# Moving the long sequence's Fourier mixing of a two-sequence encoder block to the start of the short sequence's gate and up products, through DRAM

## The chip, the cores and the metric

One core of one Trainium2 chip runs the kernel. The time is the device time of one execution in microseconds (us). TensorE does the matmuls, ScalarE (ACT in the profile), VectorE (DVE) and GpSimd (POOL) work on elements, and SyncE (SP) issues nearly all of the kernel's transfers, in one queue.

## The reference, cut to what matters

```python
def fourier_mix(u, w_fnet):            # u: (batch, positions, 512), 4 groups of 128 channels
    ug = u.reshape(b, s, FNET_GROUPS, FNET_GROUP_DIM)
    fr = jnp.fft.fftn(ug, axes=(1, 3), norm="ortho").real
    return jnp.einsum('bsgc,gcd->bsgd', fr, w_fnet).reshape(b, s, FNET_WIDTH)

def trunk(x, ...):
    h = rmsnorm(x, g_pre_mix[l])
    p = h @ w_in[l]                    # c_q | c_kv | k_rope | f_in
    a = mla(c_q, c_kv, k_rope, g_q[l], w_uq[l], g_kv[l], w_ukv[l])
    f = fourier_mix(f_in, w_fnet[l])
    mix = jnp.concatenate([a, f], axis=-1) @ w_out[l]
    x = x + rmsnorm(mix, g_post_mix[l])
    h = rmsnorm(x, g_pre_ffn[l])
    x = x + rmsnorm(conv_ffn(h, w_gate[l], w_up[l], conv_w[l], conv_b[l], w_down[l]), g_post_ffn[l])
    return x

def reference(x_prompt, x_sample, ...):   # (1, 1024, 1024) and (1, 512, 1024), float32
    return trunk(x_prompt, ...), trunk(x_sample, ...)
```

The two requests share the weights and nothing else. The model width is 1024, there are 8 heads, and the feed-forward width is 2816.

## The kernel before, in words

The request of 1024 positions is called long, that of 512 short. Every float32 product is three matmuls of halves: `split` (L103 to L105) rounds a tile to fp32r on ACT (the `hi` half) and subtracts it from the tile on POOL or DVE (the `lo` half); hi times hi, hi times lo and lo times hi are summed in PSUM. So each operand costs one cast of ACT and one subtraction of POOL or DVE before TensorE can use it. All tiles live in one pool of 51 pages of 4 KB a partition (`pg`); PSUM has four one-bank tiles (`ps1`) and two two-bank tiles (`ps2`). The program is written in one order of Python calls; the Tile framework then sets each engine's order of instructions from it with a scheduler of its own, and puts in the waits. Each engine runs its instructions in that order. SP issues loads and stores in its order as well, and a load or store that has to wait holds up those behind it.

The program goes through these stages.

1. Input projection of short and of the two halves of long (`in_products`, L231). `in_finish` (L240) leaves long's Fourier input folded: `fs` and `fd`, the sums and differences of mirrored positions, two pages each (L267, L268). Short's Fourier mixing runs between the blocks of the last part (`between0` to `between3`).
2. The preparation of attention: `key_rope`, the load of `w_ukv` and `w_uq`, their splits (`prep_attention_kv`, `prep_attention_q` with sixteen small copies that rearrange the heads, L452 to L455), the values of short (`attention_values`, L472 to L474, `pv`, `vc`).
3. **Long's Fourier mixing.** Three tables `tr` are loaded (`fourier_load`) and split into `th`, `tl`; `fourier_fold` (L334) makes `ff` on POOL; `fourier_operand` splits `fd` and `ff` into `eh`, `el`. For each of four channel groups, `fourier_positions` (L350 to L352, `py`) multiplies by the tables, `yh` and `yl` (L371, L372) split the result, and `fourier_channels` (L383 to L385, `pv`, `pu`, `px`) multiplies by the group's matrices A and B (`abh`, `abl`); L394 to L405 put the output `fT` together, which is stored to `mixT` in DRAM. `prep_attention_q` and `attention_keys` are called after the second of these steps.
4. Attention of short and then of long (`scores`, L541; the maximum `mx` of a block, L544, is the first thing that DVE does with a block's scores), with `w_out` loaded and split during long's last heads (`wload`, `wsplit`, list `wo`), and short's output projection (`mix_short`) at its end.
5. Short's gate and up products: 22 units (`ShortGateUp.unit`, L777), each a gate product and an up product of 24 matmuls of 512 columns. A weight is loaded and split three products ahead (`AHEAD`), gate weights on POOL and up weights on DVE. The dictionary `steps` puts other work ahead of a unit: step 1 loads the first half of long's mixed activations (`mix_load`, four tiles `mtr`), step 2 splits them (`mth`, `mtl`), steps 3 to 6 are long's eight blocks of the output projection (L674, `pm`), steps 8 to 19 make and split the left operands of long's gate and up products.
6. Long's gate and up products (`LongGateUp`, L858) and the down products of both (`Down`, L1003).

Of the kernel before, what the change touches and what calls it, by code (L numbers as in the profile page):

```python
# [9 lines left out]
F32 = mybir.dt.float32  # L10
# [34 lines left out]
def kernel(  # L45
# [41 lines left out]
    def store(dst, src):  # L87
        nc.sync.dma_start(dst, src)
# [67 lines left out]
    def seq(x, y, S, tdft, name):  # L156
        q = Ctx()
        q.x, q.y, q.S, q.tdft, q.name = x[0], y[0], S, tdft, name
        q.C = S // 512
        q.KB = S // P  # L160
        q.mixT = dr.tile([D, S], F32, name=f"mixT_{name}")
        q.x1 = dr.tile([S, D], F32, name=f"x1_{name}")
        q.c = [[None] * q.C for _ in range(4)]
        q.kr = None
        q.vc, q.ks, q.qt = {}, [], {}
        q.xf = {}
        q.fold, q.traw, q.tab, q.ops = {}, {}, {}, {}
        return q


# [69 lines left out]
    def in_finish(q, c, b, o, cb):  # L240
        pc, pf = o
        if b % 2 == 0:
            cb.page = pg([P, 2, 512], F32, "cn")
        cn = cb.page[:, b % 2, :]
        ss = small("ss2", 2)
        for i in range(2):
            hs = slice(i * LORA, (i + 1) * LORA)
            nc.scalar.activation(cn[:, hs], pc[:, hs], AF.Square, accum_out=ss[:, i:i + 1])
        r = rstd(ss, LORA, 2)
        for i in range(2):  # L250
            hs = slice(i * LORA, (i + 1) * LORA)
            nc.vector.tensor_scalar(out=cn[:, hs], in0=pc[:, hs], scalar1=r[:, i:i + 1], scalar2=None, op0=ALU.mult)
        cb.append(cn)
        tb = c * 4 + b
        half = q.KB // 2
        if tb < half:
            if tb % 2 == 0:
                q.xf[tb // 2] = pg([P, 2, 512], F32, "xf")
            nc.scalar.copy(q.xf[tb // 2][:, tb % 2, :], pf)
        else:  # L260
            n = tb - half
            xf = q.xf[n // 2][:, n % 2, :]
            i, j = n // 2, n % 2
            if j == 0:
                q.fold["s", i] = pg([P, 2, 512], F32, "fs")
                q.fold["d", i] = pg([P, 2, 512], F32, "fd")
            nc.vector.tensor_tensor(out=q.fold["s", i][:, j, :], in0=pf, in1=xf, op=ALU.add)  # L267
            nc.vector.tensor_tensor(out=q.fold["d", i][:, j, :], in0=xf, in1=pf, op=ALU.subtract)  # L268

    def key_rope(q, c, w, hT, cs4):  # L270
        pk = ps1("pk")
# [18 lines left out]

    def prep_fourier():

        w = Ctx()
        tb = pg([P, 2, P], F32, "dft")
        load(tb, t_dft.rearrange("t p c -> p t c"))
        wf = pg([P, GROUPS, P], F32, "wf")
        load(wf, w_fnet.rearrange("g p c -> p g c"))
        raw = pg([P, 2, GROUPS * P], F32, "abr")
        for i in range(2):
            pa = ps1("pa")  # L300
            mm(pa, tb[:, i, :], wf.rearrange("p g c -> p (g c)"), start=True, stop=True)
            nc.scalar.copy(raw[:, i, :], pa)
        w.hi = pg([P, 2, GROUPS * P], F32R, "abh")
        w.lo = pg([P, 2, GROUPS * P], F32R, "abl")
        split(w.hi, w.lo, raw)
        return w

    def fourier_load(q, n):
        raw = pg([P, 2, q.tdft.shape[3]], F32, "tr")
# [860 lines left out]
    def between2():  # L1170
        for f in fs[3:7]:
            f()
        load_attention(wkvr, w_ukv, NOPE + 64)
        for n in (0, 2):
            fourier_load(long, n)

    def between3():
        fourier_fold(long)
        fs[7]()

    wf, wkvr, wqr = [], [], []
# [1 line left out]
    for i, (q, c) in enumerate(chunks):  # L1183
# [27 lines left out]
            transpose_c(q, c, cb)  # L1211
        km = key_rope(q, c, win, cur, cs4)
        prev = (q, c, cb, km)
    fourier_load(long, 1)
    load_attention(wqr, w_uq, NOPE + ROPE)
    wa = Ctx()
    prep_attention_kv(wa, wkvr)
    fourier_table(long, 0)
    fourier_operand(long, ("d", 0))
    fourier_table(long, 2)  # L1220
    for key in "eo":
        fourier_operand(long, key)
    attention_values(short, wa)
    key_rope_finish(prev[0], prev[1], prev[3])
    fourier_table(long, 1)
    fourier_operand(long, ("d", 1))
    for i, f in enumerate(fourier_steps(long, wf[0])):
        f()
        if i == 1:
            prep_attention_q(wa, wqr)  # L1230
            attention_keys(short)
    project_k(short, wa, 0)
    project_q(short, wa, ORDER[0])
    gb1 = broadcast_gain(g_post_mix)
# [41 lines left out]

    hb = ([], [])
    steps = {}
    steps[1] = [lambda: box.update(mr=mix_load(long, 0))]
    steps[2] = [lambda: box.update(mt=mix_operands(box["mr"]))]  # L1280

    def blocks(c, bs):
        for b in bs:
# [5 lines left out]
        box["mt"] = mix_operands(raws)  # L1289
        hb[0].append(out_finish(long, 0, 3, pm, gb1))  # L1290

    steps[3] = [lambda: blocks(0, range(2))]
    steps[4] = [lambda: blocks(0, (2,)), last_block]
    steps[5] = [lambda: blocks(1, range(2))]
    steps[6] = [lambda: blocks(1, range(2, 4))]
    for kk in range(4):
        steps[8 + 3 * kk] = [lambda kk=kk: gu_long.left(kk, hb)]
        steps[9 + 3 * kk] = [lambda kk=kk: gu_long.left_operands(kk, slice(0, 4))]
        steps[10 + 3 * kk] = [lambda kk=kk: gu_long.left_operands(kk, slice(4, 7))]
    steps.setdefault(NJ - 2, []).append(lambda: gu_long.fetch(0))  # L1300
    steps.setdefault(NJ - 1, []).extend([lambda: [f() for f in gu_long.weight_steps(0)], lambda: gu_long.fetch(1)])
    for j in range(NJ):
# [74 lines left out]
```

## Time and profile before

| | |
|---|---|
| Time, median of 3 runs | 1695.25 us (1695.03 to 1699.75) |
| The profiled execution | 1696.39 us, of which its span is 1694.6 us |
| TensorE busy | 1653.6 us of the span (98%) |
| VectorE, GpSimd, ScalarE busy | 1045.6, 900.6 and 751.8 us (62%, 53%, 44%) |
| Chain that ended last | 87% TensorE, 4% VectorE, 3% issue, 2% ScalarE, 2% GpSimd, 1% DMA |
| Moved | 193.38 MB, 114 GB/s on the mean |

The profile is of one execution. Busy time of an engine is the time in which it had an instruction under way. The start of each instruction, what it waited for, and the granted clock of TensorE in a stretch (1.00 is 2.4 GHz; at the lower level, 1.2 GHz, a row shows 0.50 or, where the stretch takes in some of both, a value between) come from the same trace. Line numbers are those of the kernel before.

### The profile page before, as it was taken

The page shows a single profiled execution, that of the slowest core. Times are in us where ns is not written, and L with a number is a line of the kernel's source. Part 1 is how long each engine was busy: PE and PEld are TensorE (multiplying, and loading weights), DVE is VectorE, ACT ScalarE, POOL GpSimd, SP SyncE. Part 2 cuts the span into 40 slices and gives each one's busy share as a digit, 9 for nine tenths or more (in the row PEclk, how much of TensorE's full clock was granted, in tenths as well). Part 3 has the DMA queues.
Part 4 walks back from the last instruction along what each step waited for, and adds up shares of the span by engine and source line. Part 5 has one row for each costly group of instructions (what it writes and reads, how often), then busy time and mean ns, then how long its engine had stood idle before and what let it go on. Part 6 is the DMA issues. An engine that isn't in the chain of part 4 may idle for free.

```text
span 1694.6 us, 21125 instructions
## 1 busy us (share of the span) xinstructions
PE 1653.6 (98%) x7686; PEld 1359.1 (80%) x7686; DVE 1045.6 (62%) x1242; ACT 751.8 (44%) x1274; POOL 900.6 (53%) x646
## 2 busy tenths in 40 slices
PE   8999889999999999999999999999999999999998
PEld 6888767788887777888888888888888887888886
DVE  4333768878887454434666576676667669723547
ACT  5332546666777343323444334333333335532432
POOL 3111436768778413311443777777777626635755
PEclk9999999999999999999999999999999999999999
DMA  6000310000003344535344434333344467645536
GB/s 242 26 8 14 131 63 10 13 11 10 22 23 131 106 128 127 178 97 146 112 126 126 125 93 118 100 94 97 103 119 117 138 214 263 217 147 190 199 132 248
DMA packets 170717, 193.38 MB, mean 114 GB/s; under 512 B 9994, under 2 KB 120822, under 8 KB 170614
## 3 DMA queue, kind: packets, MB, share of 16 engines
q1 hardware_dynamic: 169654, 190.21, 35.7%
q10 hardware_dynamic: 960, 1.84, 0.3%
q8 instruction: 60, 0.98, 0.2%
q14 instruction: 43, 0.35, 0.1%
HBM read 142.86 MB, written 49.15 MB: 113 GB/s over the span
## 4 chain that ended last, share of the span: by engine, by line
PE 87%; DVE 4%; issue 3%; ACT 2%; POOL 2%; DMA 1%; DVEq 0%; SPq 0%; POOLq 0%; ACTq 0%
PE po L1003 16%; PE pm L674 8%; PE pc L231 8%; PE mx L858 7%; PE mz L858 7%; PE my L858 7%; PE gate L777 7%; PE up L777 7%; PE sc L541 5%; PE mv L858 4%; PE pt L553 3%; PE pa L561 2%; PE pa L562 2%; ACT pr L545 1%; DVE pT L556 1%
## 5 line engine op out<-in xcount | busy, mean ns | idle before, releaser
L1003 PE MATMUL po<-bw,aw 128*128 128x512 f32 x924 | 219.7, 390 | 0.0
L1003 PEld LDWEIGHTS po<-bw,aw 128*128 128x128 f32 x924 | 173.4, 188 | 36.0
L142 POOL TENSOR_TENSOR r<-v,mhalf 128x1 f32<-128x1 f32 (+1 forms) x60 | 40.0, 669 | 260.6 <-DVE v L140 260.5
L548 POOL TENSOR_TENSOR pr<-pr,rs 128x1024 f32<-128x1024 f32 (+1 forms) x96 | 155.6, 1622 | 7.1
L858 PE MATMUL my<-hl,wx 128*128 128x512 f32 x528 | 128.6, 389 | 0.0
L858 PE MATMUL mz<-hl,wx 128*128 128x512 f32 x528 | 126.9, 389 | 0.0
L858 PE MATMUL mx<-hl,wx 128*128 128x512 f32 x528 | 126.9, 389 | 0.0
L105 POOL TENSOR_TENSOR wl<-wr,wh 128x1024 fp32r<-128x1024 f32 x22 | 53.9, 2449 | 131.1 <-ACT wh L104 125.6
L105 POOL TENSOR_TENSOR wx<-wr,wx 128x512 fp32r<-128x512 f32 x44 | 75.9, 1725 | 88.5 <-ACT wx L104 88.4
L556 DVE TENSOR_TENSOR pT<-pt,pT 128x512 fp32r<-128x512 f32 x160 | 104.9, 684 | 25.0 <-ACT pT L555 23.4
L105 DVE TENSOR_TENSOR aw<-raw,aw 128x1024 fp32r<-128x1024 f32 (+1 forms) x41 | 65.2, 1589 | 89.4 <-ACT aw L104 67.5
L1003 PE MATMUL po<-bw,an 128*128 128x512 f32 x462 | 115.9, 390 | 1.2 <-POOL bw L105 0.7
L858 PEld LDWEIGHTS my<-hl,wx 128*128 128x128 f32 x528 | 99.2, 188 | 20.5
L858 PEld LDWEIGHTS mx<-hl,wx 128*128 128x128 f32 x528 | 99.1, 188 | 20.5
L858 PEld LDWEIGHTS mz<-hl,wx 128*128 128x128 f32 x528 | 99.1, 188 | 20.5
L544 DVE TENSOR_REDUCE mx<-sc 128x1 f32<-128x1024 f32 (+1 forms) x96 | 99.3, 1041 | 23.5 <-PE sc L541 23.0
L777 PE MATMUL gate<-h2T,wh 128*128 128x512 f32 x352 | 110.9, 393 | 0.0
L105 POOL TENSOR_TENSOR bw<-rb,bw 128x512 fp32r<-128x512 f32 x44 | 71.7, 1647 | 69.6 <-ACT bw L104 69.5
L777 PE MATMUL up<-h2T,wh 128*128 128x512 f32 x352 | 108.4, 389 | 0.0
L555 ACT CAST pT<-pt 128x512 fp32r<-128x512 f32 x160 | 90.1, 590 | 39.6 <-PE pt L553 38.4
L231 PE MATMUL pc<-winh,hT 128*128 128x512 f32 x368 | 106.1, 399 | 1.1 <-ACT hT L217 0.5
L547 POOL TENSOR_TENSOR rs<-sm,mone 128x1 f32<-128x1 f32 x96 | 60.1, 627 | 88.2 <-ACT pr L545 83.4
(262 smaller groups left out, 3965.3 us busy)
## 6 DMA issues: line engine op xcount, KB each, us to landing
wr<-in_w_gate_dram SPq DMA_DIRECT2D x44, 512.0 KB, 4.2
wr<-in_w_up_dram SPq DMA_DIRECT2D x44, 512.0 KB, 6.0
raw<-left SPq DMA_DIRECT2D x76, 256.0 KB, 3.8
rb<-in_w_down_dram SPq DMA_DIRECT2D x55, 256.0 KB, 4.0
rb<-in_w_down_dram SPq DMA_DIRECT2D x22, 512.0 KB, 5.1
left<-sa SPq DMA_DIRECT2D x20, 512.0 KB
ran<-left SPq DMA_DIRECT2D x77, 128.0 KB, 3.6
xb<-in_x_prompt_dram SPq DMA_DIRECT2D x16, 512.0 KB, 5.4
```

The source lines that it names most:

```text
L105: (lo_eng or nc.gpsimd).tensor_tensor(out=lo, in0=src, in1=f32(hi), op=ALU.subtract)
L231: mm(o[i], hT[k][:, part, s], ww[:, i * 512:(i + 1) * 512], start=(k == 0 and part == 0 and ww is wh), stop=(k == KT - 1 and part == 1))
L541: mm(sc[:, hs], st[:, s], mv[:, hs], start=a, stop=z)
L544: nc.vector.tensor_reduce(out=mx, in_=sc[:, 0:S], op=ALU.max, axis=AX.X, negate=True)
L547: nc.gpsimd.tensor_tensor(out=rs, in0=sm, in1=mone, op=ALU.pow)
L548: nc.gpsimd.tensor_tensor(out=pr, in0=pr, in1=rs.to_broadcast([P, S]), op=ALU.mult)
L555: nc.scalar.copy(t[:, 0, :], pt)
L556: nc.vector.tensor_tensor(out=t[:, 1, :], in0=pt, in1=f32(t[:, 0, :]), op=ALU.subtract)
L674: mm(pm[:, hs], st[:, s], mv[:, hs], start=(k == 0 and st is ah and mv is wh), stop=(k == KT - 1 and st is al))
L777: mm(o, st[:, k, :], self.q.h2[k][0][:, part, :], start=(k == 0 and st is hi and part == 0), stop=(k == KT - 1 and st is lo))
L858: mm(o, w[:, wp, s], a[:, ap, :], start=(start and kk == 0 and wp == 0 and ap == 0), stop=(stop and kk == 3 and wp == 1), skip_group_check ...
L1003: mm(o, st[:, s], w[:, wp, :], start=(start and st is ah and wp == 0), stop=(stop and st is al), skip_group_check=True)
```

## The change

Long's folded Fourier input (four pages) and the product `raw` of the channel matrices are stored to DRAM when they are made. Long's Fourier mixing is taken out of the place between the preparation of attention and attention; `prep_attention_q` and `attention_keys` follow the values directly. Ahead of unit 0 of short's gate and up products the four folded pages (`fr`), the channel matrices (`abr`) and the three tables (`tr`) are loaded, eight transfers of 512 KB, and their folds and splits are called; two, three and three of the eight Fourier steps (four position and four channel products) stand ahead of units 1, 2 and 3. The split halves of `w_out` are given up after short's projection, and `w_out` is loaded and split a second time at steps 3 to 7. Long's mixed activations are loaded at step 6 instead of 1 and split at 7 instead of 2, the eight blocks of the output projection stand at steps 8 to 11 instead of 3 to 6, and the left operands at steps 12 to 19, two steps for each of four parts instead of three. In the new numbering L366 to L368 are the position products, L488 to L490 the values, L690 `pm` and L793 the gate and up products.

```diff
...
         q.fold, q.traw, q.tab, q.ops = {}, {}, {}, {}
+        q.kept = dr.tile([q.KB // 2, P, 1024], F32, name=f"fold_{name}")
         return q
...
             nc.vector.tensor_tensor(out=q.fold["d", i][:, j, :], in0=xf, in1=pf, op=ALU.subtract)
+            if j and q.C == 2:
+                for z, key in enumerate("sd"):
+                    store(q.kept[2 * z + i], q.fold.pop((key, i)).rearrange("p j c -> p (j c)"))

...

-        w = Ctx()
         tb = pg([P, 2, P], F32, "dft")
...
             nc.scalar.copy(raw[:, i, :], pa)
+        store(kept_ab, raw.rearrange("p i c -> p (i c)"))
+        return fourier_channel_operands(raw)
+
+    def fourier_channel_operands(raw):
+        w = Ctx()
         w.hi = pg([P, 2, GROUPS * P], F32R, "abh")
...
         return w
+
+    kept_ab = dr.tile([P, 2 * GROUPS * P], F32, name="kept_ab")
+
+    def fourier_reload(q):
+        for z, key in enumerate("sd"):
+            for i in range(2):
+                t = q.fold[key, i] = pg([P, 2, 512], F32, "fr")
+                load(t.rearrange("p j c -> p (j c)"), q.kept[2 * z + i])

...
         load_attention(wkvr, w_ukv, NOPE + 64)
-        for n in (0, 2):
-            fourier_load(long, n)

     def between3():
-        fourier_fold(long)
         fs[7]()
...
         prev = (q, c, cb, km)
-    fourier_load(long, 1)
     load_attention(wqr, w_uq, NOPE + ROPE)
     wa = Ctx()
     prep_attention_kv(wa, wkvr)
-    fourier_table(long, 0)
-    fourier_operand(long, ("d", 0))
-    fourier_table(long, 2)
-    for key in "eo":
-        fourier_operand(long, key)
     attention_values(short, wa)
     key_rope_finish(prev[0], prev[1], prev[3])
-    fourier_table(long, 1)
-    fourier_operand(long, ("d", 1))
-    for i, f in enumerate(fourier_steps(long, wf[0])):
-        f()
-        if i == 1:
-            prep_attention_q(wa, wqr)
-            attention_keys(short)
+    prep_attention_q(wa, wqr)
+    attention_keys(short)
     project_k(short, wa, 0)
...
     steps = {}
-    steps[1] = [lambda: box.update(mr=mix_load(long, 0))]
-    steps[2] = [lambda: box.update(mt=mix_operands(box["mr"]))]
+
+    def fourier_begin():
+        fourier_reload(long)
+        box["ab"] = pg([P, 2, GROUPS * P], F32, "abr")
+        load(box["ab"].rearrange("p i c -> p (i c)"), kept_ab)
+        for n in (0, 2, 1):
+            fourier_load(long, n)
+
+    def fourier_first():
+        fourier_fold(long)
+        fourier_table(long, 0, nc.vector)
+        fourier_operand(long, ("d", 0))
+        fourier_table(long, 2)
+        for key in "eo":
+            fourier_operand(long, key)
+
+    def fourier_second():
+        fourier_table(long, 1)
+        fourier_operand(long, ("d", 1))
+        box["fs"] = fourier_steps(long, fourier_channel_operands(box["ab"]))
+
+    def fourier_go(n):
+        for f in box["fs"][n]:
+            f()
+
+    def wout_load(ks):
+        for k in ks:
+            wload(k)
+
+    def wout_split(ks):
+        for k in ks:
+            wsplit(k)
+
+    steps[0] = [fourier_begin, fourier_first, fourier_second, lambda: wo.clear()]
+    steps[1] = [lambda: fourier_go(slice(0, 2))]
+    steps[2] = [lambda: fourier_go(slice(2, 5))]
+    steps[3] = [lambda: fourier_go(slice(5, 8))]
+    for k in range(0, KT, 2):
+        steps.setdefault(3 + k // 2, []).append(lambda k=k: wout_load((k, k + 1)))
+        steps[4 + k // 2] = [lambda k=k: wout_split((k, k + 1))]
+    steps[6].append(lambda: box.update(mr=mix_load(long, 0)))
+    steps[7].append(lambda: box.update(mt=mix_operands(box["mr"])))

...

-    steps[3] = [lambda: blocks(0, range(2))]
-    steps[4] = [lambda: blocks(0, (2,)), last_block]
-    steps[5] = [lambda: blocks(1, range(2))]
-    steps[6] = [lambda: blocks(1, range(2, 4))]
+    steps[8] = [lambda: blocks(0, range(2))]
+    steps[9] = [lambda: blocks(0, (2,)), last_block]
+    steps[10] = [lambda: blocks(1, range(2))]
+    steps[11] = [lambda: blocks(1, range(2, 4))]
     for kk in range(4):
-        steps[8 + 3 * kk] = [lambda kk=kk: gu_long.left(kk, hb)]
-        steps[9 + 3 * kk] = [lambda kk=kk: gu_long.left_operands(kk, slice(0, 4))]
-        steps[10 + 3 * kk] = [lambda kk=kk: gu_long.left_operands(kk, slice(4, 7))]
+        steps[12 + 2 * kk] = [lambda kk=kk: gu_long.left(kk, hb), lambda kk=kk: gu_long.left_operands(kk, slice(0, 3))]
+        steps[13 + 2 * kk] = [lambda kk=kk: gu_long.left_operands(kk, slice(3, 7))]
     steps.setdefault(NJ - 2, []).append(lambda: gu_long.fetch(0))
...
```

The framework's scheduler places the instructions anew. Three places follow.

**After the values of short, on DVE.** `wv` are the halves of the value weights, `vc` the values, `el` the lower halves of long's Fourier operands, `yl` those of the position products, `wqa` the rearranged query weights. Before:

```order
L105 TENSOR_TENSOR wv_1623<-wqkvr_1472,wv_1623 128x512
L105 TENSOR_TENSOR wv_1631<-wqkvr_1474,wv_1631 128x512
L105 TENSOR_TENSOR el_1644<-fd_1131,eh_1643 128x1024
L105 TENSOR_TENSOR el_1652<-ff_1540,eh_1651 128x1024
L105 TENSOR_TENSOR el_1656<-ff_1542,eh_1655 128x1024
L478 TENSOR_TENSOR vc_1666<-pv_1659,vc_1666 128x4x128
L478 TENSOR_TENSOR vc_1676<-pv_1669,vc_1676 128x4x128
L478 TENSOR_TENSOR vc_1686<-pv_1679,vc_1686 128x4x128
L478 TENSOR_TENSOR vc_1696<-pv_1689,vc_1696 128x4x128
L105 TENSOR_TENSOR el_1707<-fd_1385,eh_1706 128x1024
L372 TENSOR_TENSOR yl_1711<-py_1712,yh_1710 128x2x2x128
L372 TENSOR_TENSOR yl_1711<-py_1713,yh_1710 128x2x256
```

With the change:

```order
L105 TENSOR_TENSOR wv_1621<-wqkvr_1478,wv_1621 128x512
L105 TENSOR_TENSOR wv_1629<-wqkvr_1480,wv_1629 128x512
L494 TENSOR_TENSOR vc_1644<-pv_1637,vc_1644 128x4x128
L494 TENSOR_TENSOR vc_1654<-pv_1647,vc_1654 128x4x128
L468 COPY wqa_1680<-wqkvr_1617 128x4x64
L469 COPY wqa_1680<-wqkvr_1617 128x4x32
L470 COPY wqa_1680<-wqkvr_1617 128x4x16
L471 COPY wqa_1680<-wqkvr_1617 128x4x16
L468 COPY wqa_1680<-wqkvr_1617 128x4x64
L494 TENSOR_TENSOR vc_1664<-pv_1657,vc_1664 128x4x128
L469 COPY wqa_1680<-wqkvr_1617 128x4x32
L470 COPY wqa_1680<-wqkvr_1617 128x4x16
```

The four `el` and the `yl` are gone from between `wv`, `vc` and `wqa`.

**At the start of short's gate and up products, on SP and TensorE.** On SP, `wr` are the gate and up weights, the first ones those of unit 1 and the gate of unit 2. Before:

```order
L88 DMA mixT_l<-at_5872 64x512
L85 DMA wr_5941<-in_w_gate_dram 128x8x128
L85 DMA wr_5947<-in_w_up_dram 128x8x128
L85 DMA wr_5983<-in_w_gate_dram 128x8x128
L85 DMA mtr_6014<-mixT_l 128x2x512
L85 DMA mtr_6016<-mixT_l 128x2x512
L85 DMA mtr_6018<-mixT_l 128x2x512
L85 DMA mtr_6020<-mixT_l 128x2x512
L85 DMA wr_6023<-in_w_up_dram 128x8x128
```

With the change:

```order
L88 DMA mixT_l<-at_5626 64x512
L85 DMA fr_5694<-fold_l 128x1024
L85 DMA fr_5696<-fold_l 128x1024
L85 DMA fr_5698<-fold_l 128x1024
L85 DMA fr_5700<-fold_l 128x1024
L85 DMA abr_5702<-kept_ab 128x1024
L85 DMA tr_5704<-in_t_dft_l_dram 128x1024
L85 DMA tr_5706<-in_t_dft_l_dram 128x1024
L85 DMA tr_5708<-in_t_dft_l_dram 128x1024
L85 DMA wr_5747<-in_w_gate_dram 128x8x128
L85 DMA wr_5753<-in_w_up_dram 128x8x128
L85 DMA wr_5789<-in_w_gate_dram 128x8x128
```

Eight loads now stand ahead of the weights of units 1 and 2, and the `mtr` are gone from here. On TensorE, the rows between the last of unit 0 and the first of unit 1 with the change; before, `gate_6022` of unit 1 follows directly:

```order
L793 MATMUL up_5788<-h2T_5691,wh_5405 128x512 x2
L793 MATMUL up_5788<-h2T_5691,wl_5406 128x512
L366 MATMUL py_5823<-th_5714,eh_5718 128x512
L367 MATMUL py_5823<-tl_5715,eh_5718 128x512
L368 MATMUL py_5823<-th_5714,el_5719 128x512
L366 MATMUL py_5823<-th_5714,eh_5718 128x512
L367 MATMUL py_5823<-tl_5715,eh_5718 128x512
L368 MATMUL py_5823<-th_5714,el_5719 128x512
L366 MATMUL py_5822<-th_5722,eh_5726 128x256
...
L368 MATMUL py_5855<-th_5734,el_5739 128x512
L793 MATMUL gate_5884<-h2T_5635,wh_5749 128x512 x2
L793 MATMUL gate_5884<-h2T_5635,wl_5750 128x512
```

The rows left out are of the same kind: in all 24 position products of 512 columns (`py` from `th_5714` and `th_5734` with their lower halves) and 12 of 256 (`th_5722`) stand ahead of unit 1's gate. In the same place POOL's order is two `ff`, `tl_5723`, `tl_5735`, `abl_5743`, then the lower half of unit 1's gate weights; DVE's is `tl_5715`, four `el`, then that of unit 1's up weights; ACT's is the eight upper halves, then those two weights.

**Ahead of the up weights of unit 7, on SP, with the change.** `sa` are the combined results of units 4 and 5, `wor` pages of `w_out`; the first `wr` is the gate weight of unit 7, the second its up weight:

```order
L85 DMA wr_6390<-in_w_gate_dram 128x8x128
L88 DMA left_77<-sa_6421 128x2x256
L88 DMA left_77<-sa_6422 128x2x256
L85 DMA wor_6435<-in_w_out_dram 128x1024
L85 DMA wor_6437<-in_w_out_dram 128x1024
L85 DMA mtr_6439<-mixT_l 128x2x512
L85 DMA mtr_6441<-mixT_l 128x2x512
L85 DMA mtr_6443<-mixT_l 128x2x512
L85 DMA mtr_6445<-mixT_l 128x2x512
L85 DMA wr_6448<-in_w_up_dram 128x8x128
```

Before, an up weight behind four `mtr` was that of unit 2 (the row `wr_6023` above).

## Rows read from the trace of the kernel before

**Rows 1.** The profile's page: busy time of the engines, and the chain that ended last.

```profile
PE 1653.6 (98%) x7686; PEld 1359.1 (80%) x7686; DVE 1045.6 (62%) x1242; ACT 751.8 (44%) x1274; POOL 900.6 (53%) x646
...
PE 87%; DVE 4%; issue 3%; ACT 2%; POOL 2%; DMA 1%; DVEq 0%; SPq 0%; POOLq 0%; ACTq 0%
```

**Rows 2.** Waits of TensorE from 180 to 245 us: total, times, longest.

```profile
PE py L350 <- ACT fT L405: 3.2, 1, 3.2
PE pv L473 <- DVE wv L105: 2.3, 1, 2.3
```

**Rows 3.** Stretches: length, busy us (PE, PEld, DVE, ACT, POOL), granted clock, DMA share, GB/s.

```profile
190.00:194.00 4.00, 3.70 (x9) 2.93 (x10) 4.00 (x3) 0.60 (x1) 2.47 (x1) 0.57 0.01 3
...
227.00:232.00 5.00, 4.90 (x16) 3.90 (x17) 1.95 (x6) 0.96 (x3) 0.00 (x0) 0.66 0.35 138
...
800.00:950.00 150.00, 150.00 (x688) 124.67 (x687) 89.80 (x111) 65.48 (x94) 65.87 (x37) 1.00 0.47 130
950.00:1300.00 350.00, 350.00 (x1546) 289.97 (x1545) 240.62 (x218) 129.13 (x201) 261.54 (x166) 1.00 0.35 101
```

**Rows 4.** TensorE, in order of time: start, duration, line, operation.

```profile
186.31 0.39 PE L274 MATMUL pk<-hT,krw 128*128 128x512 f32 x1
...
191.26 0.63 PE L473 MATMUL pv<-wv,cT 128*128 128x512 f32 x1
191.69 0.63 PE L474 MATMUL pv<-wv,cT 128*128 128x512 f32 x1
...
198.98 0.40 PE L351 MATMUL py<-tl,eh 128*128 128x512 f32 x1
199.21 0.39 PE L352 MATMUL py<-th,el 128*128 128x512 f32 x1
...
199.55 0.28 PE L351 MATMUL py<-tl,eh 128*128 128x256 f32 x1
199.67 0.28 PE L352 MATMUL py<-th,el 128*128 128x256 f32 x1
```

**Rows 5.** POOL, DVE and ACT between 187 and 240 us, each in order of time.

```profile
187.34 5.13 POOL L105 TENSOR_TENSOR tl<-tr,th 128x1024 fp32r<-128x1024 f32 x2
...
208.96 2.54 POOL L105 TENSOR_TENSOR wql<-wqa,wqh 128x1024 fp32r<-128x1024 f32 x1 [8.09 <-ACT wqh L104]
212.81 2.35 POOL L105 TENSOR_TENSOR wql<-wqa,wqh 128x1024 fp32r<-128x1024 f32 x1 [1.31 <-ACT wqh L104]
...
187.34 5.68 DVE L105 TENSOR_TENSOR wv<-wqkvr,wv 128x512 fp32r<-128x512 f32 x2
...
209.13 2.42 DVE L454 COPY wqa<-wqkvr 128x64 f32<-128x64 f32 x1
...
213.28 3.14 DVE L491 TENSOR_TENSOR kt<-kr,kt 64x512 fp32r<-64x512 f32 x2 [1.63 <-ACT kt L490]
...
239.64 1.29 DVE L544 TENSOR_REDUCE mx<-sc 128x1 f32<-128x512 f32 x2 [3.71 <-PE sc L541]
...
207.77 1.05 ACT L104 CAST wqh<-wqa 128x1024 fp32r<-128x1024 f32 x1 [0.44 <-DVE wqa L455]
```

**Rows 6.** From 612 to 652 us: SP, POOL, DVE, TensorE; a wait; GB/s in 40 slices.

```profile
613.75 0.47 SPq L85 DMA_DIRECT2D wr<-in_w_gate_dram  x1
...
647.33 6.70 POOL L105 TENSOR_TENSOR mtl<-mtr,mth 128x1024 fp32r<-128x1024 f32 x2
...
638.56 1.22 DVE L105 TENSOR_TENSOR wl<-wr,wh 128x1024 fp32r<-128x1024 f32 x1
...
651.69 3.42 DVE L105 TENSOR_TENSOR wl<-wr,wh 128x1024 fp32r<-128x1024 f32 x1
...
626.80 0.62 PE L777 MATMUL gate<-h2T,wh 128*128 128x512 f32 x2
...
PE pm L674 <- POOL mtl L105: 1.1, 1, 1.1
...
GB/s 0 0 136 169 313 318 306 290 309 383 387 381 387 398 317 217 22 8 0 0 0 0 0 0 0 0 0 147 262 238 327 375 273 288 330 205 135 369 201 352
```

## The prediction

> **What bounds the kernel now.** I read the page first. TensorE is busy in 98% of the span and is 87% of the chain that ended last [rows 1], so a change can gain only where TensorE idles or runs at its lower clock, and costs wherever it makes TensorE wait. The change adds and takes away no matmul. What it can gain lies in the place that it empties, and what it can lose at the places that it fills. So I read TensorE's waits and granted clock around the old place of long's Fourier mixing, then the rows of the helpers there, then the start of short's gate and up products.
>
> In the old place TensorE waits 2.3 us for the lower halves of the value weights and 3.2 us in the middle of the mixing [rows 2]. After each longer wait the granted clock is low: 0.57 in 190 to 194 us, 0.66 in 227 to 232 us [rows 3], which is mostly the 1.2 GHz level. Matmuls of 512 columns follow each other by 0.43 us there against 0.23 us at 2.4 GHz; those of 256 columns by 0.12 us [rows 4]. From 800 us on TensorE is busy all the time at a granted clock of 1.00, with DVE at 60 to 69% and POOL at 44 to 75% [rows 3]. A difference of under 0.3% (5.1 us) could not be told from no change.
>
> **What the mixing costs where it is.** A group has 18 matmuls of 512 columns (12 position, 6 channel), 12 of 256 and 3 tiny ones of about 0.11 us: 18 x 0.228 + 12 x 0.119 + 0.33 = 5.9 us, for four groups **23.7 us** at full clock, with 0.228 and 0.119 for the steps of [rows 4]. This work is wholly TensorE's and has to be paid again later: +23.7.
>
> **What taking it out gives back.** I follow one stretch, from the end of the key-rope products at 186.5 us [rows 4] to the maximum of the first scores at 239.64 us [rows 5]: 53.1 us. With the change it should run so. The 24 value products of short take 24 x 0.228 = 5.5 us; their operands `wv` took 2.8 us each because POOL was at `tl` [rows 5], and POOL is now free, so they end near 192.6. Three `vc` and eight copies of the first half of the query weights follow on DVE, through at about 195 (an estimate). From there I take the chain of before: from the first `wqh` cast at 207.77 to the end of the second `wql` at 212.81 + 2.35 took 7.4 us [rows 5], which now ends at 202.4. It contains a copy of 2.42 us that began just after POOL's `wql` and ended with it [rows 5]; its neighbours take 0.2. Then the lower halves of the keys, of which the two at 213.28 took 3.14 us, again past POOL's end [rows 5], and two from PSUM: 2.5 us, to 204.9. Twelve value products of long wait for the PSUM bank behind these keys, and start at the low clock after the idle time: between 12 x 0.228 and 12 x 0.43 us, I take 4.0, to 208.9. First scores and maximum: 1.6, to **210.5**. The stretch shrinks by 239.6 - 210.5 = **29.1 us**; with the copies and keys held up longer or less I allow 26 to 32. So the mixing costs 29.1 us where it is, 5.4 more than its work. The five added stores stand beside TensorE's input products and are costed at nothing: by 190 us the queue had nothing under way (share 0.01 [rows 3]). If they delayed `w_ukv`, the value products would be late next.
>
> **What putting it in costs.** Unit 1's gate began at 626.80 [rows 6]. Now 24 x 0.228 + 12 x 0.119 = 6.9 us of position products stand ahead of it, whose operands come from DRAM. SP issues the eight loads where it issued unit 1's weights, at 613.75 [rows 6]. What the queue carried then, summed over the slices from 614 us on, is 3.1 MB (six loads) by 624.5, 4.2 MB (eight) by 627.5 and nine by 629 [rows 6]. The first table can be cast at 624.7, after which ACT has eight casts of about 1.0 us [rows 5]: the last at 632, unit 1's gate weights at 633. Behind them stand five subtractions of DVE (1.22 us alone [rows 6]), four of POOL (2.4 us) and unit 1's up weights on DVE. The question is whether the two engines work side by side. The rows say no: beside POOL's two `mtl`, which took 6.70 us instead of about 4.9, DVE's `wl` took 3.42 us against 1.22 alone [rows 6], and `wv`, the copy and the keys above fit the same. One after another they come to 5 x 1.2 + 4 x 2.4 + 1.2 = 16.8 us from about 625.8. The last table and operand are then there at 637.2 and unit 1's gate halves at 639.5. The last twelve products run from 637.2, nine at the low clock, to 641.0. Lost to TensorE: 641.0 - 626.8 - 6.9 = **7.3 us**, of which I keep 5 to 10.
>
> The Trainium skill states this as a rule that speaks against the change: in "SBUF — State Buffer", section "Who interferes with whom", a VectorE instruction with two SBUF inputs and a GpSimd instruction that reads SBUF exclude each other for the whole instruction. This trace agrees (3.42 us against 1.22); a fold, two table halves, the channel halves and a weight on one engine against five operands on the other are all of that kind. By the rule the loss is the 7.3 above; without it, it would be the 3.5 of the second rival.
>
> **Later waits.** Products after that run closely: unit 7's up product is due at 641.0 + 13 x 5.47 (products of 24 matmuls) + 16.8 (the rest of the mixing) = 728.9. Its weights stand on SP behind the stores of unit 5, which cannot be issued before about 717, two pages of `w_out` and four `mtr`: 4.2 MB, which took 13 to 14 us at the start of this stage [rows 6]. They land at 729 to 731, and a cast and a subtraction follow: **2.5 us** late (0 to 5). The first output block of long needs `mtl` behind `wl` and `wol` on POOL; the casts and subtractions of four `mtr`, two `w_out` pages and two weights come to some 17 us in that window. I take **2.3 us** (0 to 4); the wait of 1.1 us that it had before [rows 6] goes. The second load and split of `w_out` (4 x 2.4 us of POOL, 4 x 1.22 of DVE, 8 x 1.0 of ACT) and the left operands in two steps instead of three are costed at nothing: TensorE was never idle from 800 to 1300 us, part of it with DVE at 69% and POOL at 75% [rows 3]. If that cover failed, the `hl` operands would be late next, at 1300 us, and nothing before reads them.
>
> **Sum.** 23.7 - 29.1 + 7.3 + 2.5 + 2.3 - 1.1 = **+5.6 us** on the profiled execution of 1696.39 us, 1702.0. That execution is 1.14 us above the median of 1695.25, so the median should be **1701**. Its own ends: with 26 to 32, 5 to 10, 0 to 5 and 0 to 4 it runs from -4.4 to +15.6.
>
> **Rivals.** *No late weights (1696).* The transfers of 4.2 MB are spread by the free slots of earlier units, so that unit 7's weights and the `mtl` come in time: 23.7 - 29.1 + 7.3 - 1.1 = +0.8. For it: from 630 to 638 us the queue moved nothing at all [rows 6], so there is room. Against it: SP issues in order, and the stores ahead wait for unit 5.
>
> *The other side: DVE and POOL work side by side (1689.5).* One mechanism, which decides if instructions of 1024 columns on both engines overlap. Then the copy and the keys are not held up (-2.3 us on the 29.1), unit 1's gate halves are ready at 637.2, the last position products run from 633, and the loss at the start is 637.2 - 626.8 - 6.9 = 3.5; with the later waits absent: 23.7 + 3.5 - 31.4 - 1.1 = -5.3, and -5.8 if the clock stays up. For it: `wql` took 2.54 and 2.35 us beside the copy and the keys [rows 5], so POOL at least lost nothing there. Against it: the stretched rows above.
>
> *Slower reload (1708).* The folded pages were written 440 us earlier and come back like a weight, but if the eight loads run at 300 GB/s throughout (the slices of 616 to 620 us [rows 6]) instead of rising to 390, the tables come 3 us later, and the same rate at unit 7 adds 4: +12.6.
>
> *The change does not do what it says:* the order of instructions excludes it; the position products stand ahead of unit 1.
>
> **How the numbers follow.** The forecast gets 0.37, no late weights 0.24, side by side 0.22, slower reload 0.17. Faster by over 0.3% means below 1690.2, slower above 1700.3. Side by side gives 0.18 to faster and 0.04 to same; no late weights is all same; the forecast's own band straddles the bound, 0.12 same and 0.25 slower; slower reload is slower. Together 0.18, 0.40, 0.42. The range goes from 1687, a little under the side-by-side case, to 1709, a little over the slow reload.
>
> **What would show it.** Right: the first `mx` near 210 instead of 239.6; no wait inside the values of short; between unit 0 and unit 1 waits of TensorE for `th`, `el` or `tl` that add up to some 5 us and a granted clock under 1.00 there; DVE's `el` stretched to POOL's ends; a wait of an up product of unit 7 for DMA, ACT or DVE. Wrong: the first `mx` later than 213 (then another chain than the query weights sets the end); unit 1's gate before 637 or after 644; waits of TensorE in 800 to 1300 us, which would mean that the compressed left operands or `w_out` are not hidden.

## The result: 0.9% slower, about two and a half times the forecast

| | kernel before | with the change |
|---|---|---|
| Median | 1697.5 us (4 runs, 1695.03 to 1700.26) | 1711.74 us (4 runs, 1708.97 to 1716.43) |
| Ratio | 1 | 1.0089 (95% interval 1.0070 to 1.0108) |
| Span of the profiled execution | 1694.6 us | 1714.6 us |

The sign was forecast, the size was not: +14 us between the medians where +5.6 had been worked out, and the time lies outside the range. The profiled execution with the change is the highest of its four, so the two spans differ by 20.0 us, more than the medians. What follows takes those 20.0 us apart; which of its parts are smaller in the other executions no profile shows.

The page with the change has the same engines at nearly the same shares as [rows 1]; TensorE's share of the chain fell from 87% to 85%, and DMA's rose from 1% to 3%:

```profile
PE 1663.0 (97%) x7686; PEld 1361.7 (79%) x7686; DVE 1058.7 (62%) x1247; ACT 761.5 (44%) x1283; POOL 916.6 (53%) x650
...
PE 85%; DVE 4%; DMA 3%; ACT 2%; issue 2%; POOL 2%; SPq 0%; DVEq 0%; POOLq 0%; ACTq 0%
```

TensorE's waits with the change, in the whole span. The first three rows are new, the last stood at 1.1 us before [rows 6]; other new ones are of 1.6 us and less:

```profile
PE up L793 <- ACT wh L104: 6.4, 2, 4.0
...
PE py L368 <- DVE el L105: 4.1, 4, 2.3
...
PE pv L488 <- DVE kt L525: 2.7, 1, 2.7
...
PE pm L690 <- POOL mtl L105: 0.9, 1, 0.9
```

Of the two waits of [rows 2] the one of 3.2 us is gone, and the one of 2.3 us has become 0.5. To see where the 20.0 us are, I compare the starts of the same instructions in the two traces. The first maximum stands at 213.24 us against 239.64 [rows 5]:

```profile
213.24 1.29 DVE L560 TENSOR_REDUCE mx<-sc 128x1 f32<-128x512 f32 x2 [4.30 <-PE sc L557]
```

That is 26.4 us earlier. Unit 0's first gate product and the first product of long's gate and up stand at, before:

```profile
613.57 0.47 PE L777 MATMUL gate<-h2T,wh 128*128 128x512 f32 x1
...
951.07 2.88 PE L858 MATMUL mx<-hl,wx 128*128 128x512 f32 x12
```

With the change:

```profile
587.21 0.48 PE L793 MATMUL gate<-h2T,wh 128*128 128x512 f32 x1
...
968.65 2.88 PE L874 MATMUL mx<-hl,wx 128*128 128x512 f32 x12
```

From the first maximum to unit 0's gate it is 373.9 us before and 374.0 with the change. From unit 0's gate to the first product of long's gate and up (short's gate and up stage, with long's output projection) it is 337.5 us before and 381.4 with the change: 43.9 more, of which 23.7 are the moved products. **So 20.2 us are lost in that stage.** The rest, to the end, is 743.5 and 746.0. There TensorE waits 1.0 us for a tile `m` that ACT writes, which it does not before, and the products behind it run slowly (granted clock 0.72 from 1445 to 1450 us). That the change causes these 2.5 us is not shown: the last part, the same work in all twelve kernels profiled here, took 743.4 to 746.5 us in the nine with the Fourier work moved and 743.5 to 744.8 in the three without. In sum: 23.7 - 26.4 + 20.2 + 2.5 = +20.0.

**The 20.2 us.** At the start of the stage unit 1's gate comes 28.0 us after unit 0's, against 13.2 before; less 6.9 us of products that is 7.9 lost. The subtractions of DVE and POOL in order of time:

```profile
600.16 1.22 DVE L105 TENSOR_TENSOR el<-fr,eh 128x1024 fp32r<-128x1024 f32 x1
601.86 6.20 DVE L105 TENSOR_TENSOR el<-ff,eh 128x1024 fp32r<-128x1024 f32 x2 [0.48 <-ACT eh L104]
607.98 3.39 DVE L105 TENSOR_TENSOR el<-fr,eh 128x1024 fp32r<-128x1024 f32 x1
...
606.93 3.35 POOL L105 TENSOR_TENSOR abl<-abr,abh 128x1024 fp32r<-128x1024 f32 x1
```

One `el` takes 1.22 us where no POOL instruction had begun before it and 3.39 beside POOL's, and `abl` takes 3.35 instead of 2.4: each waits for the other, as `wl` and `mtl` did in [rows 6].

Then two up products stop for their weights, in units 5 and 7, and afterwards run slowly. TensorE, and the granted clock of three stretches (length, busy us of PE, PEld, DVE, ACT, POOL, clock, DMA share, GB/s):

```profile
683.48 1.22 PE L793 MATMUL up<-h2T,wh 128*128 128x512 f32 x2 [2.34 <-ACT wh L104]
...
712.85 0.73 PE L793 MATMUL up<-h2T,wh 128*128 128x512 f32 x2 [4.02 <-ACT wh L104]
```

```profile
680.00:690.00 10.00, 7.62 (x20) 5.23 (x19) 4.55 (x6) 6.57 (x9) 3.94 (x2) 0.66 0.80 240
690.00:706.00 16.00, 16.00 (x72) 13.19 (x71) 5.97 (x8) 3.69 (x4) 6.60 (x3) 1.00 0.72 237
708.00:717.00 9.00, 4.40 (x13) 2.92 (x12) 4.01 (x6) 4.15 (x6) 1.79 (x1) 0.83 0.47 120
```

Against a step of 0.23 us the products around the first wait lose 5.9 us, those around the second 6.6: the waits are 2.3 and 4.0, with 0.6 more for the lower half `wl` in the second, and the rest is products at up to 0.43 us a step. With 1.2 us at the first output block, and 1.1 us that the kernel before lost there, 7.9 + 5.9 + 6.6 + 1.2 - 1.1 = 20.5, which agrees with 20.2.

Why the weights were late stands in SP's queue, in order of time (start, how long the issuing took with its waits):

```profile
643.87 14.87 SPq L88 DMA_DIRECT2D mixT_l<-fT  x2
658.84 1.20 SPq L85 DMA_DIRECT2D wor<-in_w_out_dram  x2
...
671.57 3.07 SPq L88 DMA_DIRECT2D left<-sa  x2
674.73 0.91 SPq L85 DMA_DIRECT2D wor<-in_w_out_dram  x2
675.72 0.38 SPq L85 DMA_DIRECT2D wr<-in_w_up_dram  x1
...
697.59 1.20 SPq L85 DMA_DIRECT2D wor<-in_w_out_dram  x2
698.88 2.87 SPq L85 DMA_DIRECT2D mtr<-mixT_l  x4
701.84 0.74 SPq L85 DMA_DIRECT2D wr<-in_w_up_dram  x1
```

Unit 5's up weights are issued at 675.72 and could be cast at 682.39, when TensorE had been idle since 681.1; unit 7's were issued at 701.84 and cast at 711.75. Ahead of the one, SP stood 14.9 us at two stores of Fourier outputs that were not there yet, and 3.1 us at stores of unit 3's results; ahead of the other are 3 MB.

The first of these stops had ended 17 us before unit 5's load. What links the two stands on ACT, DVE and POOL:

```profile
667.50 1.05 ACT L104 CAST wh<-wr 128x1024 fp32r<-128x1024 f32 x1 [6.47 <-DMA wr<-in_w_up_dram]
...
668.58 1.23 DVE L105 TENSOR_TENSOR wl<-wr,wh 128x1024 fp32r<-128x1024 f32 x1 [6.88 <-ACT wh L104]
669.72 0.68 DVE L724 TENSOR_TENSOR t<-up,t 128x512 f32<-128x512 f32 x1
...
671.57 2.67 DVE L724 TENSOR_TENSOR sa<-t,sa 128x256 f32<-128x256 f32 x1
...
671.55 2.41 POOL L105 TENSOR_TENSOR wl<-wr,wh 128x1024 fp32r<-128x1024 f32 x1 [24.25 <-DVE sa L724]
```

Unit 4's up weights, issued at 660.13 behind the Fourier stores and two pages of `w_out`, were cast at 667.50, and DVE took their subtraction ahead of unit 3's result `t`. Then `sa` took 2.67 us beside POOL's `wl`, against 0.43 in the same place of a kernel without the Fourier work here (the `w_out` part alone, below). Only then could SP store both and go on to unit 5's weights. The 2.2 us that `sa` lost are nearly as long as the wait of 2.3; that they alone made it was not tried.

### The profile page after: what moved, and what is told of

It reads as the page before. It is cut to its first block, busy times and chain, and to the rows that moved or that the text cites. A ratio compares the mean times of both kernels' runs of the same rounds, so it can differ in the third digit from the quotient of the medians.

```text
span 1714.6 us, 21177 instructions
## 1 busy us (share of the span) xinstructions
PE 1663.0 (97%) x7686; PEld 1361.7 (79%) x7686; DVE 1058.7 (62%) x1247; ACT 761.5 (44%) x1283; POOL 916.6 (53%) x650
## 4 chain that ended last, share of the span: by engine, by line
PE 85%; DVE 4%; DMA 3%; ACT 2%; issue 2%; POOL 2%; SPq 0%; DVEq 0%; POOLq 0%; ACTq 0%
PE po L1019 15%; PE pm L690 8%; PE pc L232 7%; PE my L874 7%; PE mx L874 7%; PE mz L874 7%; PE up L793 6%; PE gate L793 6%; PE sc L557 5%; PE mv L874 3%; PE pt L569 3%; PE pa L577 2%; PE pa L578 2%; DMA raw<-left 1%; DMA wr<-in_w_up_dram 1%
## 5 line engine op out<-in xcount | busy, mean ns | idle before, releaser
L572 DVE TENSOR_TENSOR pT<-pt,pT 128x512 fp32r<-128x512 f32 x160 | 104.9, 684 | 24.9 <-ACT pT L571 23.7
L793 PE MATMUL up<-h2T,wh 128*128 128x512 f32 x352 | 111.9, 400 | 6.4 <-ACT wh L104 6.4
L793 PE MATMUL gate<-h2T,wh 128*128 128x512 f32 x352 | 111.5, 394 | 0.0
L557 PE MATMUL sc<-kt,qh 128*128 128x512 f32 x352 | 102.3, 407 | 4.6 <-ACT pr L561 3.7
```

The source lines that it names most:

```text
L557: mm(sc[:, hs], st[:, s], mv[:, hs], start=a, stop=z)
L572: nc.vector.tensor_tensor(out=t[:, 1, :], in0=pt, in1=f32(t[:, 0, :]), op=ALU.subtract)
L793: mm(o, st[:, k, :], self.q.h2[k][0][:, part, :], start=(k == 0 and st is hi and part == 0), stop=(k == KT - 1 and st is lo))
```

## The experiments

The theory: three losses stand on TensorE's path, DVE and POOL holding each other up at the start, weights late behind other work in SP's order, and a chain of the query weights before the first scores. Most of the experiments take one of them away, or several together; two keep long's Fourier mixing in its old place. All ratios are to the kernel before, which was timed on the same chip in each experiment; "stage" is the time from unit 0's gate to the first long gate product (before 337.5, with the change 381.4).

| kernel | ratio (interval) | first maximum | unit 1's gate after unit 0's | stage |
|---|---|---|---|---|
| the change | 1.0089 (1.0070 to 1.0108) | 213.2 | 28.0 | 381.4 |
| restart on DVE | 1.0049 (1.0034 to 1.0064) | 211.9 | 22.3 | 373.7 |
| weights further ahead | 1.0006 (0.9997 to 1.0016) | 213.4 | 28.3 | 367.9 |
| stores from ACT | 1.0043 (1.0029 to 1.0057) | 213.4 | 28.3 | 373.7 |
| w_out part alone | 1.0032 (1.0020 to 1.0045) | 241.5 | 13.2 | 342.8 |
| query halves on DVE | 1.0068 (1.0053 to 1.0083) | 209.4 | 28.4 | 381.3 |
| old place, on DVE | 0.9984 (0.9975 to 0.9993) | 237.7 | 13.2 | 337.3 |
| one unit later | 1.0029 (1.0018 to 1.0040) | 212.7 | 13.2 | 370.2 |
| three cures | 0.9970 (0.9959 to 0.9982) | 212.1 | 22.1 | 363.9 |
| later, ahead, DVE | 0.9960 (0.9946 to 0.9973) | 210.5 | 13.2 | 361.2 |
| the same, keys first | 0.9941 (0.9928 to 0.9955) | 206.9 | 13.2 | 361.7 |

**The start of the stage on DVE alone.**

```diff
-        fourier_table(long, 2)
+        fourier_table(long, 2, nc.vector)
...
-        fourier_table(long, 1)
+        fourier_table(long, 1, nc.vector)
...
-        split(w.hi, w.lo, raw)
+        split(w.hi, w.lo, raw, nc.vector)
```

> The changed kernel with the lower halves of the last two tables and of the channel matrices subtracted on DVE instead of POOL, at the start of short's gate and up products. Theory (DVE and POOL exclude each other there, so their instructions add up; POOL takes about 2.4 us for what takes DVE 1.2): the same work in a row becomes some 5 us shorter, unit 1's first gate product starts 3 to 5 us earlier than in the changed kernel (600 + 10 to 12 instead of 615.2 us), DVE's subtractions show 1.2 us each instead of 3.4, and the time falls by 3 to 5 us against the changed kernel. Rival (the start is bound by the reload from DRAM and ACT's casts, the last of which ends at 606.6): DVE gets longer, unit 1 starts within 1 us of 615.2 or later, and the time does not fall.

Unit 1's gate came at 608.2, 5.7 us earlier relative to unit 0's, a little more than expected. DVE did more work in less time, and now POOL was the one held up, with 7.25 us for two weights of 2.4; for one of them unit 1's gate, two products in, waited 1.9 us:

```profile
603.80 1.22 DVE L105 TENSOR_TENSOR tl<-tr,th 128x1024 fp32r<-128x1024 f32 x1
604.94 1.22 DVE L105 TENSOR_TENSOR el<-fr,eh 128x1024 fp32r<-128x1024 f32 x1
606.07 1.22 DVE L105 TENSOR_TENSOR abl<-abr,abh 128x1024 fp32r<-128x1024 f32 x1
...
605.76 7.25 POOL L105 TENSOR_TENSOR wl<-wr,wh 128x1024 fp32r<-128x1024 f32 x2 [9.45 <-ACT wh L104]
...
PE gate L793 <- POOL wl L105: 1.9, 1, 1.9
```

So 3.5 us are left of the gain when unit 1's gate is done. The rival is out: the reload and ACT's casts set where the row of subtractions begins (the first cast, at 597.93 with the change), not where it ends. The waits for weights got shorter by 1.8 us too, which I had not expected; with the slow products after them that is 4.3 us, and the ratio fell by 0.0040 (6.8 us), more than expected. Why they got shorter was not looked into.

**The weights of units 2 to 11 two products further ahead.** `prepare` splits as before, but a new `fetch` loads raw weights up to two products beyond it.

```diff
-            self.prepare(self.order.index((kind, j)) + 1 + self.AHEAD)
+            self.prepare(self.order.index((kind, j)) + 1 + self.AHEAD, 2 if 2 <= j < 12 else 0)
```

> The changed kernel with the gate and up weights of units 2 to 11 loaded two products further ahead (two more pages; split as before). Theory (units 5 and 7 wait because their up weights stand on SP behind stores that wait and behind w_out and mtr pages): a load that is two products, 10.9 us, earlier lands in time, both waits of up for wh and the low clock after them go, and the time falls by 10 to 13 us against the changed kernel. Rival (the pages or the transfer rate hold the loads up, not their place): the loads wait for a page or the waits move to the next weights, and the time falls by under 4 us.

Both waits of `up` for `wh` are gone, the stage shrank by 13.5 us, the ratio by 0.0083 (14 us). This is the largest part of the miss, and the pages and the transfers allowed the earlier loads.

**Short's stores from ACT's queue.**

```diff
-            flush(1)
+            flush(1, nc.scalar)
```

> The changed kernel with the stores of short's gate and up results issued from ACT's queue instead of SP's; the loads keep their order. Theory as it stands (it is the stores waiting for DVE on SP that make unit 5's weights late): unit 5's up load is issued 4 us or more earlier and its wait goes (6 us less); unit 7's gets smaller by 1 to 4 us; in all 6 to 10 us less than the changed kernel. Rival (it is the 1 and 3 MB of w_out and mtr ahead of the weights that make them late): both waits stay within 1 us of 2.4 and 4.0, and the time stays within 2 us of the changed kernel; ACT waiting for DVE's results could add a little.

Unit 5's wait is gone; unit 7's is half as long:

```profile
PE up L793 <- ACT wh L104: 2.0, 1, 2.0
```

So the theory holds for unit 5, and for unit 7 in part. What is left at unit 7 has another cause than the pages ahead of its weights: SP, done with the four mixed pages at 693.1, could issue the weights only at 700.3, when a store of `sa` from ACT's queue was through:

```profile
SPq L85 <- DMA left<-sa: 7.5, 2, 7.2
```

**The w_out part alone.** Long's Fourier mixing as in the kernel before; `wo.clear()` at step 0, and steps 3 to 19 as with the change.

> One part of the change alone: long's Fourier mixing stays in its old place, and only the second load and split of w_out and the later places of long's output blocks and left operands are taken over. Theory (units 5 and 7 wait because of the stores, the w_out and the mtr pages ahead of their weights on SP, whatever stands at the start): up products of units 4 to 7 wait for their weights as in the changed kernel, 4 to 13 us with the low clock after them, and the time is 1703 to 1712, a ratio of 1.002 to 1.008. Rival (it is the Fourier outputs' stores, for which SP waited some 20 us in this stage, that made those weights late): no wait of an up product over 0.6 us, and the time is within 3 us of the kernel before.

Only unit 7 waits, 2.9 us, and with the low clock after it the stage is 5.3 us longer. Neither expectation is met whole: unit 7 is late with or without the Fourier work, unit 5 only with it.

```profile
PE up L777 <- ACT wh L104: 2.9, 1, 2.9
```

With the experiment before, this gives two causes: for unit 5 the stores that SP waits for, and for unit 7 what stands ahead of its weights, the stores of unit 5's results and 3 MB of `w_out` and mixed pages. How much of unit 7's wait is the pages' is argued, not shown: no run took them away. Each of these two kernels lacks one of the two kinds of stores there, and unit 5 waits in neither; this one lacks the Fourier products too, so their stores alone were not tried.

**The query weights' lower halves on DVE.**

```diff
-            split(hi, lo, arr)
+            split(hi, lo, arr, nc.vector)
```

> The changed kernel with the lower halves of the query weights subtracted on DVE instead of POOL, between the values of short and the first scores. Theory (the chain from the first wqh to the keys' lower halves sets the end of this stretch, and POOL's two subtractions hold DVE's copy and keys up): the copy of 2.4 us takes 0.2, the two keys' halves 1.3 in place of 3.2, and the first maximum comes 3 to 5 us before 213.2; the time falls by 3 to 5 us. Rival (the chain is only as long as its instructions, with no exclusion): 2 x 1.2 us less, and 2.4 us more on DVE ahead of the keys: no change within 1 us.

The first maximum came 3.9 us earlier and the ratio fell by 0.0021 (3.6 us), inside what was expected, though the intervals of the two ratios overlap; and not only for the reason given. The copy took 0.18 us and the two keys' halves 1.40, as the theory has it. Yet DVE now had 2.4 us more to do, and the long value products began only 1.2 us earlier. The rest is the clock. TensorE waits for the same thing in both, 2.73 us here and 2.68 with the change:

```profile
205.20:209.00 3.80, 3.80 (x17) 3.13 (x18) 1.87 (x3) 1.21 (x2) 0.00 (x0) 1.00 0.00 0
```

The same products with the change:

```profile
206.40:211.60 5.20, 5.20 (x12) 4.08 (x13) 1.86 (x3) 1.20 (x2) 0.00 (x0) 0.50 0.00 0
```

**The old place with the tables' and query weights' lower halves on DVE** (in the kernel before).

> The kernel before, with the Fourier mixing in its old place, and the lower halves of long's three tables and of the query weights subtracted on DVE instead of POOL. Theory (a part of what the change gained at the old place came from POOL and DVE no longer holding each other up, and can be had without the move): the wait of 2.3 us for the value weights and the low clock after it go, the wait of 3.2 us gets shorter, and the kernel before gets 3 to 7 us faster. Rival (the old place is bound by the order of products and casts): under 2 us, or slower, as DVE has five more instructions there.

The wait for the value weights fell from 2.3 to 0.2 us, but one of 2.0 us for `vc` took its place, and the 3.2 us became 2.6:

```profile
PE py L350 <- ACT fT L405: 2.6, 1, 2.6
PE pk L283 <- DVE vc L478: 2.0, 1, 2.0
```

The first maximum came 1.9 us earlier, as the rival has it; the time fell by 0.16% (2.7 us, 1.2 to 4.2 by the interval), between the two. Of the 26.4 us that the change gains up to the first maximum, 23.7 are the moved products, so what it gains net there is 2.7, and 1.9 of that were to be had at the old place by another choice of engine.

**Everything one unit later.** `gu_short.prepare(4)` ahead of the reload, so that unit 1's weights are loaded first; Fourier products at steps 2 to 4, and all that follows one step later.

> The changed kernel with unit 1's weights loaded ahead of the eight reloads and everything from the Fourier products to the left operands one unit later; engines and places of the splits as in the changed kernel. Theory (the loss at the start is the time that the reload, the casts and the mutually exclusive subtractions need, and 11 us of unit 1's products cover it): unit 1's gate starts about 13 us after unit 0's as before, no wait of py over 1 us, the loss of 7.9 us falls to under 2, and the time falls by 5 to 8 us; the waits of two up products behind w_out and mtr stay, in later units. Rival (the weights of unit 2, now behind the reloads, or the page pool take the wait over): the time falls by under 3 us.

Unit 1's gate is back at 13.2 us after unit 0's, and no `py` waits over 0.8 us. The ratio fell by 0.0060 (10 us): more than the 7.9 lost there, because both long waits of `up` for `wh` went as well, which I had expected to stay. A wait of `pm` for `mtl` came instead:

```profile
PE pm L690 <- POOL mtl L105: 4.2, 1, 4.2
```

**Together.**

> The changed kernel with three cures together: the restart's subtractions on DVE, the weights of units 2 to 11 loaded two products further ahead, and the query weights' lower halves on DVE. Theory (three separate losses, each on TensorE's path): the savings add up, 7.0 at the start, 13.4 at units 5 and 7 and 4.1 before the first scores, so that the first long gate product comes at 968.6 - 24.5 = 944 us (951.1 in the kernel before) and the time is about 1692, 0.4% under the kernel before. Rival (one limit behind them all, such as the transfers, takes over): less than 17 us saved, and no gain on the kernel before.

> The changed kernel with everything from the Fourier products on one unit later (unit 1's weights ahead of the reloads), the weights of units 2 to 12 loaded two products further ahead, and the query weights' lower halves on DVE. Theory: 7 saved at the start, 13.4 at the two up products and 4.1 before the first scores; first long gate product at about 944 us, the time about 1692, 0.4% under the kernel before. Rival: the fetch further ahead fills the queue with weights where the reloads should run, and 3 to 7 us of the gain at the start are lost again.

Both are faster than the kernel before. The three cures saved 18.8 us to the first long gate product instead of 24.5, the shifted version 23.1. In the first, 1.9 us of waiting for POOL's `wl` stayed, and the long value products ran at the low clock again. In the second the stage takes 361.2 us, 23.7 more than before: just the moved products, with no loss beyond what the kernel before had there.

**Keys ahead of the query weights,** on top of the second.

```diff
-    prep_attention_q(wa, wqr)
     attention_keys(short)
+    prep_attention_q(wa, wqr)
```

> The version with the shift, the early fetch and the query weights' lower halves on DVE, with the keys' upper and lower halves called ahead of the query weights. Theory (TensorE's wait of 2.7 us for the keys' lower halves, with the low clock after it, comes from DVE's order, in which they stand behind the second half of the query weights): that wait falls under 1.5 us, the first maximum comes 2 to 4 us earlier than in that version, the first long gate product at 942 to 944 us, and the time is about 1689. Rival (the second query weights set the end of the stretch anyway): the wait moves to pq for wql, and the first maximum stays within 1 us.

The wait is gone and the first maximum is 3.6 us earlier. At 1687.89 us (5 runs, 1687.79 to 1688.18) this is the fastest version, 0.6% under the kernel before. Up to the first maximum it is 32.8 us ahead of the kernel before, 9.0 more than the moved products. How much of that needs the move is not shown: keys ahead of the query weights was not tried with the Fourier mixing in its old place.

## Why the forecast had the sign right and the size wrong

- **The work moved, +23.7: right.** The version without loss in the stage grew by 23.7. (The sum as written, four times 5.86, gives 23.4.)
- **What the old place gives back, -29.1: too much by 2.7.** The chain came as followed, to `wql` at 202.9 (202.4 forecast); the products behind the keys began at 206.4 instead of 204.9, and all twelve ran at 1.2 GHz, 5.2 us instead of 4.0. So the first maximum, at 213.24, lies just past the 213 that was named as a sign of another chain, and yet the chain was the one forecast.
- **The start of the stage, +7.3: right**, 7.9 measured, and for the reason given; the Trainium skill's rule in "SBUF — State Buffer", section "Who interferes with whom", held in the rows shown here (3.39 us beside, 1.22 alone). The rival of engines side by side is out, and so is the slower reload: the first table was cast 10.7 us after unit 0's gate, with 11.1 forecast. Two readings in that working are off: the last twelve products, nine of them at 0.43 us and three at 0.228, take 4.6 us and not the 3.8 from 637.2 to 641.0, which would have made the loss 8.0; and the slices of [rows 6] hold 4.3 MB, eight loads and not nine.
- **Later waits, +2.5 for unit 7: the step that failed.** It measured 6.6, and 5.9 more at unit 5, which the forecast did not have: 10.0 us of the miss. Two things were wrong. It priced a late load by the wait alone (2.5, against 4.0 measured and 2.9 with the `w_out` part alone), though the same text had counted the low clock at the start. And it followed SP's queue only at the place with the most bytes: the Fourier stores stand ahead of `w_out` in it, and they could not be issued before the channel products, now spread among the products of units 2 and 3, were done. That the second load and split of `w_out` "are costed at nothing" held for the splits and not for the loads' place in the queue: with the `w_out` part alone the stage is 5.3 us longer.
- **The first output block, +2.3: 1.2.** Between 850 and 960 us TensorE is busy all the time with the change too, so the compressed left operands cost nothing there, as said.
- With these, 5.6 + 2.7 + 0.6 + 10.0 - 1.1 = 17.8, against 17.6 measured up to the first long gate product. With the 2.5 us of the last part that is the 20 us of the profiled execution; the medians are 14.2 apart.

## What to carry to other kernels

When transfers are moved, write out the queue's whole order over the stretch, with the time at which each store's data exist: here stores that waited up to 14.9 us held up the loads behind them, and loading two products further ahead cost two pages and saved 14 us. A wait of TensorE can cost more than its length, here up to two and a half times; price the products after it. Where two engines hold each other up over a row of work, as DVE and POOL did here, try giving it to the faster one: it paid at the start of this stage, until POOL's remaining share became the wait.

## What the runs showed that was not expected

The clock after the same wait was not the same in three executions. In three kernels with the same instructions in this stretch TensorE waits 2.73 us for the keys' halves. Then twelve products ran wholly at 2.4 GHz in one (0.23 us a step, granted clock 1.00), from the seventh on at 1.2 GHz in another, and wholly at 1.2 GHz (0.43 us a step) in the third. That is 0 to 2.4 us for one wait. It may be part of why runs of one of these kernels spread over several us: the four runs of the change order by their mean granted clock, 1716.43 us at 0.991, 1712.40 at 0.993, 1711.08 at 0.994 and 1708.97 at 0.995, and the five of the fastest version, which has no wait there, stand at 0.998 and 0.999 and spread over 0.4 us. That this one cause makes the difference was not tried.
